# The row factors' tile moves to the place of a padding, and VectorE applies the first chunk's norm factors

## The chip, the cores and the metric

The kernel runs on one core of a Trainium2 chip. What counts is the device time of one execution in microseconds (us), as the median of several runs. One further execution was profiled.

## The reference, cut to what matters

Two transformer blocks of depth 2 are applied to 256 tokens of width 1024, all in float32. The first block normalises its input, and this is where the change to the arithmetic's place lies:

```python
def layer_norm(x, g, b):
    mu = jnp.mean(x, -1, keepdims=True)
    var = jnp.mean(jnp.square(x - mu), -1, keepdims=True)
    return (x - mu) * lax.rsqrt(var + LN_EPS) * g + b

x = layer_norm(x, ln_in_g, ln_in_b)
for l in range(DEPTH):                       # first block
    proj = einsum('bsd,de->bse', x, w_in[l]) # 1024 x 6816
    ...  # three attentions of proj's parts, gates, w_branch, w_out, layer_norm
    gu = einsum('bsd,df->bsf', x, w_ffn_in[l])
    ...  # silu(gate) * up, w_ffn_out, layer_norm
for i in range(DEPTH):                       # second block
    ...  # the same in outline: rms_norm, w_in_2, attention, gating, w_o,
    ...  # rms_norm, w_up, convolution over tokens, w_down
```

All matrix products with weights are the bulk of the work: some 257 MB of float32 weights are read once.

## The kernel before

**Matrix products.** Each weight product is done in three matmuls of a faster float32 type, on operands that are split in a high part (ScalarE casts, L188) and a low part (VectorE subtracts, L192): high with high (L254), high with low (L255), low with high (L256), all in `mm3`. The activations, turned so that the 1024 features lie on the partitions, are the tiles `xh` and `xl` (x^T, high and low), 128 x 8 x 256 elements each. The weights come by DMA into one of three `raw` tiles and are split into tiles of the pool `s4` (30 buffers of 4608 bytes a partition).

There are two kinds of product, and which operand is loaded into the array (stationary) and which streams through it (moving) differs:

- `gemm_a`: the activations are stationary (128 x 128 pieces), the weights move, 512 columns at a time (384, 288 or 256 for some narrow parts). The profile names these `ps<-s,xh` and `ps<-s,xl` where the activations are x^T, and `ps<-s,s` where they are another tile of the pool `s4` (the FFN's hidden layer, the merged attention).
- `gemm_b`: the weights are stationary, the activations move, 256 columns (all tokens) at a time. The profile names these `ps<-xh,s` and `ps<-xl,s`, or `ps<-s,s` where the activations are an attention's output in `s4` (the product with `w_branch`). Here the split weights start 64 bytes (high) or 192 bytes (low) into their `s4` buffer (`OFF_HI`, `OFF_LO`).

The order of the steps is written out by the program itself: a list of steps, each issued to the engines in turn, with the splitting of weights a fixed number of units ahead. Between the products of an attention's softmax chain, weight products are placed as filler.

**Where the tiles lie.** The pools are laid out one behind the other, and every tile starts at a multiple of 32 bytes. In the program of the kernel before, the bytes of a partition at which the tiles start are:

```
x_tok     2176     xh       10368     xl       18560     fixed    26752
pad      29376     neghalf  29408     ones     29504     col      29536
row      31328     neglam   31360     raw      31392  (and + 8192 each)
s4       55968  (and + 4608 each)     s2      194208     g, b    218784
```

`pad` is a tile of 8 floats that nothing reads or writes. `row` holds two floats a partition, the factors of the two halves of the rows in the second block's norms.

**The start.** `head` writes out the first steps: the statistics of the first 128 rows (VectorE L493, L516; GpSimd L361, L362), their norm (L523), eight transposes by TensorE (L530, two chunks of four, each chunk a PSUM bank), the cast of the first weight unit (`high(0)`, ScalarE L188), then `in_high(0, 0)`: factor and bias of the first chunk (ScalarE L537, four pieces of 128 columns) and its cast into `xh` (ScalarE L538). Only then VectorE is given the statistics of the second 128 rows (`in_stats(1)`), the low part of the first weight unit (`low_next`, L192) and that of the first chunk (`in_low(0, 0)`, L542). The same functions serve the other three chunks later.

Of the kernel before, what the change touches and what calls it, by code (L numbers as in the profile page):

```python
# [10 lines left out]
F32 = mybir.dt.float32  # L11
F32R = mybir.dt.float32r
AF = mybir.ActivationFunctionType
ALU = mybir.AluOpType
# [3 lines left out]
P = 128  # L18
# [8 lines left out]
RMS_EPS = 1e-6  # L27
MASKED = -1e30

X_PAD = 8
WARM = (0, 0)

RAW_BUFS = 3
S4_BUFS = 30
# [79 lines left out]
class Net:  # L116
# [295 lines left out]
    def constants(self):  # L412
        nc, a, cp = self.nc, self.a, self.cp
        self.x_tok = cp.tile([P, 2, D], F32, name="x_tok")
        self.xh = cp.tile([P, KT, 256], F32R, name="xh")
        self.xl = cp.tile([P, KT, 256], F32R, name="xl")
        self.fixed = cp.tile([P, a["c_fixed"].shape[1]], F32, name="fixed")
        cp.tile([P, X_PAD], F32, name="pad")
        self.neghalf = cp.tile([P, 20], F32, name="neghalf")
        nc.vector.memset(self.neghalf, -0.5)  # L420
        self.ones = cp.tile([P, 1], F32, name="ones")
        nc.vector.memset(self.ones, 1.0)
        self.col = cp.tile([P, a["c_vectors"].shape[1]], F32, name="col")
        self.row = cp.tile([P, 2], F32, name="row")
        self.neglam = cp.tile([P, DEPTH], F32, name="neglam")
        for c in range(2):
            cs = slice(c * 512, c * 512 + 512)
            nc.sync.dma_start(self.x_tok[:, 0, cs], a["x"][0, :P, cs])
        nc.sync.dma_start(self.fixed[:, :P + 2 * KT], a["c_fixed"][:, :P + 2 * KT])
        self.ident = self.fixed[:, :P]  # L430
        self.ln_in = [self.fixed[:, P + i * KT:P + (i + 1) * KT] for i in range(2)]
        o = P + 2 * KT

        def table(n):
            nonlocal o
            o += 4 * n
            return self.fixed[:, o - 4 * n:o].rearrange("p (a t n) -> p a t n", a=2, t=2)

        self.rope_df, self.rope_mla, self.rope_gqa = table(16), table(32), table(64)
        self.mask = self.fixed[:, o:o + 64]  # L440
# [91 lines left out]
    def in_high(self, t, c):  # L532
        nc, y, ps = self.nc, self.s2([P, 4, P]), self.in_ps[t, c]
        self.in_y[t, c] = y
        for k in range(4):
            g, b = (v[:, 4 * c + k:4 * c + k + 1] for v in self.ln_in)
            nc.scalar.activation(y[:, k, :], ps[:, k * P:k * P + P], AF.Identity, scale=g, bias=b)  # L537
        nc.scalar.copy(self.xh[:, 4 * c:4 * c + 4, t * P:t * P + P], y)  # L538

    def in_low(self, t, c):  # L540
        ks, ts = slice(4 * c, 4 * c + 4), slice(t * P, t * P + P)
        self.nc.vector.tensor_tensor(self.xl[:, ks, ts], self.in_y[t, c], self.xh[:, ks, ts], op=ALU.subtract)  # L542

    def warm(self, n):

        for _ in range(n):
            self.nc.tensor.matmul(self.warm_ps[:, :P], self.warm_in, self.warm_in, start=True, stop=True)

    def head(self, dfq, dfk):


        self.in_scale, self.in_ps, self.in_y = {}, {}, {}

        def first():
            if WARM[0]:
                self.warm_in, self.warm_ps = self.s2([P, P]), self.psum()
                self.nc.gpsimd.memset(self.warm_in, 1.0)
            self.warm(WARM[0])
            self.in_stats(0)
            self.in_norm(0)  # L560
            self.in_trans(0)
            self.warm(WARM[1])
            self.high(0)
            self.in_high(0, 0)
            self.in_stats(1)
            self.low_next()
            self.in_low(0, 0)
            self.high(1)
            self.low_next()
            self.in_high(0, 1)  # L570
            self.in_norm(1)
            self.in_low(0, 1)

        def second():
            self.in_trans(1)
            self.high(2)
            self.low_next()
            self.high(3)

        def third():  # L580
            self.in_high(1, 0)
            self.low_next()
            self.in_low(1, 0)
            self.in_high(1, 1)

        self.add(first, dfq[:2], second, dfq[2], third, dfq[3], lambda: self.in_low(1, 1), self.lookahead(AHEAD_EDGE), dfq[4:], dfk)

    def in_rows(self, t):
# [837 lines left out]
```

## Time and profile before

| | |
|---|---|
| median of 3 runs | 1506.68 us (1506.45 to 1506.7) |
| profiled execution | 1504.22 us, of which the span from the first to the last instruction is 1502.4 us |
| TensorE busy | 1478.0 us, 98% of the span |
| VectorE / ScalarE busy | 990.2 us (66%) / 822.8 us (55%) |
| granted TensorE clock, mean | 0.998 |

Busy time of TensorE is the time in which at least one matmul is in flight. Matmuls overlap in the pipeline, so the duration shown for one matmul is longer than the distance from its start to the next one's start; that distance is what counts where they follow one another without a wait.

### The profile page before, as it was taken

To read this page: it belongs to the slowest core of one execution; us is meant where nothing else is said; L and a number is where in the kernel's file an instruction comes from. 1 tells how busy PE (TensorE), PEld (TensorE's weight loads), DVE (VectorE), ACT (ScalarE), POOL (GpSimd) and SP (SyncE) were. 2 spreads that over 40 slices of the span, in tenths; PEclk is the share of its full clock that TensorE was granted. 3 is DMA by queue.
4 is the path that set the end of the run, shared out by engine and by line. 5 is a ranking of instruction groups with operands and counts; after the bars stand their busy time and mean duration, and the time that the engine had idled before them with its cause. 6 is when DMAs were issued, how large, how long until landed. Compare 5 with 4: busy or idle time off the path is not lost.

```text
span 1502.4 us, 23794 instructions
## 1 busy us (share of the span) xinstructions
PE 1478.0 (98%) x9616; PEld 1314.7 (88%) x9616; DVE 990.2 (66%) x1434; ACT 822.8 (55%) x1387; POOL 90.3 (6%) x116
## 2 busy tenths in 40 slices
PE   7999999999999999999999999999999999999998
PEld 5889988899988889998889998777999887789987
DVE  5786655855556676556775555876788758669881
ACT  6664566444442565656444443675767536568660
POOL 0000020000000000011000000310000012000000
PEclk9999999999999999999999999999999999999999
DMA  7744565576563654466665564553565735255660
GB/s 242 249 138 153 177 115 177 168 225 196 193 229 98 203 162 141 147 146 169 201 224 182 178 215 140 183 180 113 164 199 194 254 124 193 74 168 169 199 222 28
DMA packets 179021, 260.44 MB, mean 173 GB/s; under 512 B 23648, under 2 KB 122208, under 8 KB 178912
## 3 DMA queue, kind: packets, MB, share of 16 engines
q1 hardware_dynamic: 178912, 258.93, 54.4%
q8 instruction: 75, 1.23, 0.3%
q14 instruction: 34, 0.28, 0.1%
HBM read 257.86 MB, written 1.05 MB: 172 GB/s over the span
## 4 chain that ended last, share of the span: by engine, by line
PE 48%; DVE 3%; ACT 0%; issue 0%; POOL 0%; DVEq 0%; POOLq 0%; ACTq 0%
PE ps L254 15%; PE ps L256 15%; PE ps L255 15%; DVE s L192 1%; PE ps L1142 1%; PE ps L390 1%; PE ps L406 1%; PE ps L642 0%; DVE x_tok L505 0%; DVE st L493 0%; PE ps L1191 0%; DVE s L492 0%; PE ps L1298 0%; PE ps L1181 0%; DVE s L913 0%
## 5 line engine op out<-in xcount | busy, mean ns | idle before, releaser
L192 DVE TENSOR_TENSOR s<-raw,s 128x1024 fp32r<-128x1024 f32 (+2 forms) x468 | 553.9, 1211 | 175.4 <-ACT s L188 126.6
L188 ACT CAST s<-raw 128x1024 fp32r<-128x1024 f32 (+2 forms) x468 | 466.3, 1039 | 117.1 <-PE ps L255 26.4
L254 PE MATMUL ps<-xh,s 128*128 128x256 f32 x1664 | 475.6, 286 | 1.9 <-DVE s L738 1.4
L255 PE MATMUL ps<-xl,s 128*128 128x256 f32 x1664 | 468.0, 281 | 0.0
L256 PE MATMUL ps<-xh,s 128*128 128x256 f32 x1664 | 466.4, 280 | 0.0
L254 PEld LDWEIGHTS ps<-xh,s 128*128 128x128 f32 x1664 | 313.2, 188 | 10.1 <-issue 6.5
L255 PEld LDWEIGHTS ps<-xl,s 128*128 128x128 f32 x1664 | 317.7, 191 | 0.5
L256 PEld LDWEIGHTS ps<-xh,s 128*128 128x128 f32 x1664 | 314.0, 189 | 0.0
L254 PE MATMUL ps<-s,s 128*128 128x512 f32 (+1 forms) x712 | 259.4, 364 | 0.0
L255 PE MATMUL ps<-s,s 128*128 128x512 f32 (+1 forms) x712 | 254.6, 358 | 0.0
L256 PE MATMUL ps<-s,s 128*128 128x512 f32 (+1 forms) x712 | 254.4, 357 | 0.0
L254 PE MATMUL ps<-s,xh 128*128 128x512 f32 (+3 forms) x448 | 171.8, 383 | 3.6 <-ACT xh L538 3.2
L256 PE MATMUL ps<-s,xl 128*128 128x512 f32 (+3 forms) x448 | 169.6, 379 | 1.0 <-DVE xl L351 1.0
L255 PE MATMUL ps<-s,xh 128*128 128x512 f32 (+3 forms) x448 | 169.2, 378 | 0.0
L254 PEld LDWEIGHTS ps<-s,s 128*128 128x128 f32 x712 | 133.7, 188 | 29.2 <-issue 10.0
L256 PEld LDWEIGHTS ps<-s,s 128*128 128x128 f32 x712 | 133.7, 188 | 20.5
L255 PEld LDWEIGHTS ps<-s,s 128*128 128x128 f32 x712 | 133.8, 188 | 18.4
L254 PEld LDWEIGHTS ps<-s,xh 128*128 128x128 f32 x448 | 84.6, 189 | 20.0 <-ACT xh L538 3.6
L256 PEld LDWEIGHTS ps<-s,xl 128*128 128x128 f32 x448 | 84.5, 189 | 19.5 <-DVE xl L351 3.0
L255 PEld LDWEIGHTS ps<-s,xh 128*128 128x128 f32 x448 | 84.7, 189 | 15.8 <-DVE s L192 0.5
L361 POOL TENSOR_SCALAR st<-st 128x2 f32<-128x2 f32 (+2 forms) x46 | 24.2, 525 | 963.6 <-DVE st L500 456.9
L400 ACT ACTIVATE s<-ps,st 128x256 f32<-128x256 f32 x96 | 44.6, 472 | 50.2 <-DVE st L397 49.7
(177 smaller groups left out, 1253.6 us busy)
## 6 DMA issues: line engine op xcount, KB each, us to landing
raw<-in_w_in SPq DMA_DIRECT2D x61, 1024.0 KB, 5.2
raw<-in_w_ffn_in SPq DMA_DIRECT2D x88, 512.0 KB, 5.1
raw<-in_w_up SPq DMA_DIRECT2D x88, 512.0 KB, 5.0
raw<-in_w_ffn_out SPq DMA_DIRECT2D x22, 1024.0 KB, 5.0
raw<-in_w_down SPq DMA_DIRECT2D x22, 1024.0 KB, 5.0
raw<-in_w_branch SPq DMA_DIRECT2D x12, 1024.0 KB, 5.3
raw<-in_w_out SPq DMA_DIRECT2D x8, 1024.0 KB, 5.0
raw<-in_w_o SPq DMA_DIRECT2D x8, 1024.0 KB, 5.0
```

The source lines that it names most:

```text
L188: nc.scalar.copy(u.hi, u.raw.tile[:, u.off:u.off + u.nk, :])
L192: nc.vector.tensor_tensor(u.lo, u.raw.tile[:, u.off:u.off + u.nk, :], u.hi, op=ALU.subtract)
L254: mm(out, lh, rh, start=first, stop=False, skip_group_check=skip)
L255: mm(out, lh, rl, start=False, stop=False, skip_group_check=skip)
L256: mm(out, ll, rh, start=False, stop=last, skip_group_check=skip)
L361: self.nc.gpsimd.tensor_scalar(v, src, scale, eps, op0=ALU.mult, op1=ALU.add)
L390: self.nc.tensor.matmul(o[r, :256], vs[:, r] if vs.shape[1] == P else vs, pts[i][:, k * 256:k * 256 + 256], start=k == 0, stop=k == 1)
L400: nc.scalar.activation(p[:, qs], src[:, qs], AF.Exp, bias=nmx[:, q:q + 1], accum_out=sm[:, q:q + 1])
L406: self.nc.tensor.transpose(ps[:, k * 256 + q * P:k * 256 + q * P + P], p[:, q * 256 + k * P:q * 256 + k * P + P], self.ident)
L1142: nc.tensor.matmul(ps[:, q * 256:q * 256 + 256], S["qT"][r, h % 4, q * P:q * P + P], S["kT"][r, :], start=True, stop=True)
```

## The change

The padding tile and its size are removed, and the tile `row` is allocated where the padding was. In `in_high`, for the first chunk of the first rows alone, the factor and the bias are applied by two VectorE instructions over all 512 columns in the place of four ScalarE instructions. A function that issued warm-up matmuls, with counts of (0, 0), is removed with its constants.

```diff
-X_PAD = 8
-WARM = (0, 0)
...
         self.fixed = cp.tile([P, a["c_fixed"].shape[1]], F32, name="fixed")
-        cp.tile([P, X_PAD], F32, name="pad")
+        self.row = cp.tile([P, 2], F32, name="row")
         self.neghalf = cp.tile([P, 20], F32, name="neghalf")
...
         self.col = cp.tile([P, a["c_vectors"].shape[1]], F32, name="col")
-        self.row = cp.tile([P, 2], F32, name="row")
         self.neglam = cp.tile([P, DEPTH], F32, name="neglam")
...
     def in_high(self, t, c):
         nc, y, ps = self.nc, self.s2([P, 4, P]), self.in_ps[t, c]
         self.in_y[t, c] = y
-        for k in range(4):
-            g, b = (v[:, 4 * c + k:4 * c + k + 1] for v in self.ln_in)
-            nc.scalar.activation(y[:, k, :], ps[:, k * P:k * P + P], AF.Identity, scale=g, bias=b)
+        if t == c == 0:
+            g, b = (v[:, :4].unsqueeze(2).broadcast_to([P, 4, P]) for v in self.ln_in)
+            nc.vector.tensor_tensor(y, ps.rearrange("p (k n) -> p k n", k=4), g, op=ALU.mult)
+            nc.vector.tensor_tensor(y, y, b, op=ALU.add)
+        else:
+            for k in range(4):
+                g, b = (v[:, 4 * c + k:4 * c + k + 1] for v in self.ln_in)
+                nc.scalar.activation(y[:, k, :], ps[:, k * P:k * P + P], AF.Identity, scale=g, bias=b)
         nc.scalar.copy(self.xh[:, 4 * c:4 * c + 4, t * P:t * P + P], y)
...
-    def warm(self, n):
-        for _ in range(n):
-            self.nc.tensor.matmul(self.warm_ps[:, :P], self.warm_in, self.warm_in, start=True, stop=True)
...
-            if WARM[0]:
-                self.warm_in, self.warm_ps = self.s2([P, P]), self.psum()
-                self.nc.gpsimd.memset(self.warm_in, 1.0)
-            self.warm(WARM[0])
             self.in_stats(0)
             self.in_norm(0)
             self.in_trans(0)
-            self.warm(WARM[1])
             self.high(0)
             self.in_high(0, 0)
             self.in_stats(1)
```

## Rows read from the trace of the kernel before

**Rows 1.** Page, part 1: busy us of each engine, share of the span.

```profile
PE 1478.0 (98%) x9616; PEld 1314.7 (88%) x9616; DVE 990.2 (66%) x1434; ACT 822.8 (55%) x1387; POOL 90.3 (6%) x116
```

**Rows 2.** Matmuls of `mm3` by line and shape: count, busy us, mean ns.

```profile
L254 PE MATMUL ps<-xh,s 128*128 128x256 f32 x1664 | 475.6, 286 | 1.9 <-DVE s L738 1.4 <-ACT s L738 0.5
...
L254 PE MATMUL ps<-s,s 128*128 128x512 f32 x508 | 201.6, 397 | 0.0
...
L254 PE MATMUL ps<-s,xh 128*128 128x512 f32 x352 | 142.1, 404 | 3.6 <-ACT xh L538 3.2 <-ACT xh L350 0.4
...
L254 PE MATMUL ps<-s,s 128*128 128x256 f32 x204 | 57.8, 284 | 0.0
...
L254 PE MATMUL ps<-s,xh 128*128 128x384 f32 x32 | 10.8, 337 | 0.0
...
L254 PE MATMUL ps<-s,xh 128*128 128x288 f32 x32 | 9.5, 296 | 0.0
```

**Rows 3.** TensorE's timeline, first and last rows of four stretches: start, us, instruction.

```profile
25.77 0.39 PE L255 MATMUL ps<-s,xh 128*128 128x512 f32 x1
...
36.97 0.39 PE L255 MATMUL ps<-s,xh 128*128 128x512 f32 x1
...
258.76 0.28 PE L254 MATMUL ps<-s,s 128*128 128x256 f32 x1
...
267.94 0.28 PE L254 MATMUL ps<-s,s 128*128 128x256 f32 x1
...
379.77 0.28 PE L255 MATMUL ps<-xl,s 128*128 128x256 f32 x1
...
398.97 0.28 PE L256 MATMUL ps<-xh,s 128*128 128x256 f32 x1
...
439.73 0.39 PE L256 MATMUL ps<-s,s 128*128 128x512 f32 x1
...
469.87 0.39 PE L254 MATMUL ps<-s,s 128*128 128x512 f32 x1
```

**Rows 4.** Timeline around the largest wait of TensorE behind the start.

```profile
231.75 1.05 ACT L188 CAST s<-raw 128x1024 fp32r<-128x1024 f32 x1 [3.96 <-DMA raw<-in_w_branch]
...
234.25 0.95 PE L406 MATMUL ps<-fixed,s 128*128 128x128 f32 x4 [1.96 <-ACT s L829]
```

**Rows 5.** Windows: length, busy us of each engine, granted clock, DMA share, GB/s.

```profile
235.70:239.20 3.50, 3.50 (x15) 2.85 (x14) 0.50 (x2) 2.56 (x6) 0.76 (x1) 0.52 0.95 359
...
1060.00:1150.00 90.00, 90.00 (x768) 90.00 (x767) 74.26 (x121) 66.55 (x102) 0.00 (x0) 1.00 0.54 174
```

**Rows 6.** Timeline of the start.

```profile
6.74 1.97 PE L530 MATMUL ps<-fixed,x_tok 128*128 128x128 f32 x8 [6.74 <-DVE x_tok L523]
8.74 1.04 ACT L188 CAST s<-raw 128x1024 fp32r<-128x1024 f32 x1 [6.75 <-DMA raw<-in_w_in]
9.70 1.50 ACT L537 ACTIVATE s<-ps,fixed 128x128 f32<-128x128 f32 x4
10.03 1.29 DVE L493 BATCH_NORM_STATS2 st<-x_tok 128x6 f32<-128x512 f32 x2 [2.89 <-DMA x_tok<-in_x]
11.23 0.62 ACT L538 CAST xh<-s 128x512 fp32r<-128x512 f32 x1
...
11.48 1.18 DVE L192 TENSOR_TENSOR s<-raw,s 128x1024 fp32r<-128x1024 f32 x1
...
11.90 0.80 PE L254 MATMUL ps<-s,xh 128*128 128x512 f32 x1 [3.20 <-ACT xh L538]
12.58 0.68 DVE L542 TENSOR_TENSOR xl<-s,xh 128x512 fp32r<-128x512 f32 x1
...
12.71 0.80 PE L255 MATMUL ps<-s,xh 128*128 128x512 f32 x1
...
13.31 0.79 PE L256 MATMUL ps<-s,xl 128*128 128x512 f32 x1
```

**Rows 7.** VectorE's groups by shape: a 512-column operation with a PSUM operand.

```profile
L351 DVE TENSOR_TENSOR xl<-ps,xh 128x512 fp32r<-128x512 f32 x28 | 17.9, 683 | 11.0 <-ACT xh L350 11.0
```

## The prediction

> **What bounds the kernel now.** I read the page's busy times first: TensorE is busy for 1478.0 us, 98% of the span [rows 1]. Of the span's 1502.4 us that leaves 24.4 without a matmul, near half of it before the first product at 11.90 [rows 6]. So what changes the time by more than a few us is the distance between matmuls that follow each other without a wait, and I looked there next.
>
> The groups of matmuls by shape give the counts, and the timeline of TensorE gives the distances. In [rows 3] the reader is to divide the time from the first to the last start of a stretch by the starts in between:
>
> - weights moving, x^T stationary, 512 columns: 25.77 to 36.97 us, 49 rows, 11.20 / 48 = 233.3 ns;
> - weights moving, another `s4` tile stationary, 512 columns: 439.73 to 469.87, 134 rows, 30.14 / 133 = 226.6 ns;
> - x^T moving, weights stationary, 256 columns: 379.77 to 398.97, 164 rows, 19.20 / 163 = 117.8 ns;
> - `s4` tile moving, weights stationary, 256 columns: 258.76 to 267.94, 82 rows, 9.18 / 81 = 113.3 ns.
>
> The same instruction in the same loop is 6.7 ns (512 columns) or 4.5 ns (256 columns) slower if one of its operands is x^T. None of the four stretches has a wait, so no other engine's delay makes the difference. What differs is where the operands lie. With the starts listed above taken modulo 64 bytes, x^T lies at 0 (10368 and 18560), every `s4` buffer at 32 (55968, and 4608 is a multiple of 64), and the offsets 64 and 192 within it keep that. The two slow kinds have one operand at 0 and one at 32; the two fast kinds have both at 32. A rule that fits all four: a matmul is slower if its moving operand and the stationary operand that is loaded meanwhile are out of step by 32 bytes modulo 64.
>
> **The change part by part.**
>
> *The tile's place.* `pad` has 32 bytes; `row` has 8, and with every tile at a multiple of 32 it takes the same 32. So `neghalf`, `ones` and `col` stay. Behind `col` the old `row` is gone: `neglam` and all pools (`raw`, `s4`, `s2`, `g`, `b`, `st`) move down by 32 bytes, and `s4` starts at 55936, which is 0 modulo 64. Against x^T the `s4` buffers then lie exactly as `s4` buffers lie against one another: distance 0 modulo 512 in `gemm_a`, 64 and 192 in `gemm_b`, the distances of the two fast stretches. So I forecast that matmuls with x^T take the fast distances:
>
> - 256 columns, x^T moving: 1664 on each of three lines [rows 2], 4992 x 4.5 ns = 22.5 us;
> - 512 columns, x^T stationary: 352 x 3 = 1056 x 6.7 ns = 7.1 us;
> - the narrow ones (384 and 288 columns, 32 x 3 each [rows 2], and a third narrow kind about as many): 288 matmuls; no stretch shows their fast form, so between nothing and 6.7 ns each, 0 to 1.9 us; I take 1.2, since they lie between the two widths whose gains are 4.5 and 6.7.
>
> The products of `s4` with `s4` keep their distance modulo 512 and so their pace.
>
> From this 30.8 us something is given back. Filler between the steps of a softmax chain gets shorter, and where the chain or a transfer is what ends last, the wait grows. [rows 4] show such a place: ScalarE stood 3.96 us for a weight transfer, and TensorE behind it 1.96 us. About 1,540 of the 4,992 matmuls lie in the attentions, worth 6.9 us; I take 2 us of it as lost, between 0 and all 6.9. Elsewhere the engines that feed TensorE have room: in the densest stretch of the second block's FFN VectorE is busy 74.26 of 90 us [rows 5], 82.5%, and the same work in 4% less time would be 86%.
>
> Here a rule speaks against this part. The Trainium skill (TensorE: Matmul & The Clock Gate, section "Step-by-step: what each phase is for") says that TensorE reads moving and stationary operands through two independent ports and that loading the next weights takes nothing from the running matmul. By that rule the operands' places don't matter and this part would be worth 0. The trace disagrees as far as the 226.6 against 233.3 ns above show; what no row shows is a matmul with both operands at 0.
>
> *Factor and bias by VectorE.* Removed: four ScalarE instructions, 1.50 us. Added: two on VectorE over 512 columns, one with a PSUM operand, at 0.683 us each [rows 7], 1.37 us. In the start [rows 6] ScalarE takes them up behind the weight cast, 9.70 to 11.20, then the cast into `xh`, 0.62, and TensorE starts its first product at 11.90. After the change VectorE can start when the first chunk's transposes end (about half of 6.74 to 8.71, so 7.7) and is done near 9.1; ScalarE casts `xh` right behind the weight cast, 9.8 to 10.4, and the first matmul starts near 10.45, 1.45 us earlier. But the second matmul (L255) needs the low part of the weights, which VectorE makes from 11.48 to 12.66, and the third (L256) the low part of the chunk, ready at 13.26. Both stand on VectorE behind the statistics of the second rows, which wait for a transfer that lands at 10.03. That chain doesn't move. So L255 stays at 12.71, L256 at 13.31, and what follows with them: worth 0. The two new instructions are hidden by VectorE's idle 2.89 us before 10.03; with that cover gone they would cost 1.37. ScalarE is free 1.5 us earlier for the second weight unit, whose low part still waits for VectorE. Bounds: 1.45 us gained to 1.37 lost.
>
> *The warm-up function* issued nothing at counts of (0, 0): 0.
>
> **Sum.** 22.5 + 7.1 + 1.2 - 2.0 + 0 = 28.8 us less. The profiled execution took 1504.22 us (1502.4 of span), 2.5 us under the median of the runs, 1506.68; the sum is a difference and I set it against the median: 1477.9, told as 1478. One thing of that size is in neither: a stretch at half clock (0.52 granted in 235.70 to 239.20 [rows 5], and a second like it near 700 us), behind waits as in [rows 4]. 3.5 us at half the rate cost 1.75; none, one or three of them may be left.
>
> **The rivals.**
>
> *The place doesn't matter.* x^T matmuls are slow for a reason that moves with x^T. For it: the rule of two ports, named above, and that no x^T operand is seen at another place. Against it: the pairs differ in nothing else, and `s4` buffers far apart and close together all have the fast distance. Then all that is left is the start: 1506.7 less 0 to 1.45, about 1506.4.
>
> *Slower: a start at 0 modulo 64 is itself what costs.* The four stretches are fitted by a second rule too: fast only if no operand lies at 0. Then after the change every operand lies there; x^T matmuls gain nothing, and the products of `s4` with `s4` fall to the slow distances: 508 x 3 x 6.7 ns = 10.2 us and 204 x 3 x 4.5 ns = 2.8 us [rows 2], so 1506.7 + 13.0 = 1519.7. It decides as soon as the 512-column products of the FFN's second half stand at 233 ns. For it: no matmul of these rows has both at 0. Against it: two reads that disturb each other should depend on their distance, and moving both by 32 bytes leaves that as it is.
>
> **How the numbers follow.** The forecast has 0.68, no effect of the place 0.13, the slower rule 0.19. Under about 0.2% (3 us) a measurement of this kernel tells nothing from no change; the start alone stays under that. So faster 0.68, same 0.13, slower 0.19. The forecast's own range is 1472 (all 30.8 us kept, both half-clock stretches gone: 1506.7 - 30.8 - 3.5) to 1485 (all 6.9 us of the attentions lost and one more half-clock stretch: 1477.9 + 4.9 + 1.75). To leave out no more than 2 in 10, the range takes in the case of no effect: 1472 to 1507.
>
> **What would show it.** Right: from start to start, 256-column matmuls with x^T near 113.3 ns and 512-column ones near 226.6, `s4` products unchanged; the first L254 near 10.45 us with L255 still near 12.7; the DVE chain from 10.03 unmoved. Wrong: x^T matmuls still at 117.8 and 233.3 (place without effect), or `s4` products at 233 (the second rule), or fast matmuls with TensorE's waits risen by as much as they gained (a chain or the transfers bound it). If L255 starts with L254 near 11, the low part didn't wait as I read it.

## The result, and the profile after

The changed kernel took 1483.10 us (median of 3 runs, 1482.66 to 1484.14) against 1506.68: a ratio of 0.9845, 95% interval 0.9823 to 0.9868. The forecast was 1478, in the range of 1472 to 1507. The profiled execution took 1484.14 us with a span of 1482.3, against 1504.22 and 1502.4 before: 20.1 us less in this pair of profiles, 23.6 us in the medians. The working below explains the pair of profiles. Executions of one kernel spread with TensorE's granted clock: the 55 runs of the kernel before in the experiments below took 1500.2 to 1503.9 us where its mean was 0.999 or more, and 1506.5 to 1511.5 us where it was 0.995, so that a difference of 2 or 3 us between medians of a few runs tells little.

First the page's busy times and its group of 256-column products with x^T moving (count, busy us, mean ns):

```profile
PE 1453.9 (98%) x9616; PEld 1294.3 (87%) x9616; DVE 989.4 (67%) x1436; ACT 820.8 (55%) x1383; POOL 90.2 (6%) x116
...
L250 PE MATMUL ps<-xh,s 128*128 128x256 f32 x1664 | 467.0, 281 | 1.9 <-DVE s L729 1.4
```

The same 9616 matmuls keep TensorE busy for 24.1 us less than in [rows 1], and the group's mean fell from 286 to 281 ns [rows 2]. That mean mixes waits and pace, so the timeline is needed. First and last rows of the four kinds of stretch, as in [rows 3] (start, us, instruction; `mm3`'s lines are now 250 to 252):

```profile
257.74 0.28 PE L250 MATMUL ps<-s,s 128*128 128x256 f32 x1
...
266.92 0.28 PE L250 MATMUL ps<-s,s 128*128 128x256 f32 x1
...
292.24 0.39 PE L250 MATMUL ps<-s,xh 128*128 128x512 f32 x1
...
297.00 0.39 PE L250 MATMUL ps<-s,xh 128*128 128x512 f32 x1
...
379.81 0.28 PE L250 MATMUL ps<-xh,s 128*128 128x256 f32 x1
...
398.96 0.28 PE L251 MATMUL ps<-xl,s 128*128 128x256 f32 x1
...
438.66 0.39 PE L250 MATMUL ps<-s,s 128*128 128x512 f32 x1
...
468.81 0.39 PE L251 MATMUL ps<-s,s 128*128 128x512 f32 x1
```

From start to start: `s4` tile moving 9.18 / 81 = 113.3 ns (82 rows; as before), x^T stationary 4.76 / 21 = 226.7 (22 rows; before 233.3), x^T moving 19.15 / 169 = 113.3 (170 rows; before 117.8), `s4` stationary 30.15 / 133 = 226.7 (134 rows; as before). The x^T products of these two shapes have taken the pace of the others, and the products of `s4` with `s4` kept theirs. With this the rival of no effect (117.8 and 233.3 left) and the slower rival (`s4` products at 233 with a start at 0 modulo 64) are both out.

Both profiles issue the same matmuls in the same order, so each distance from one start to the next can be paired with its counterpart, and the changes summed by kind:

| kind of distance | us | forecast |
|---|---|---|
| x^T moving, 256 columns (4845 at a steady pace, 89 beside waits or at half clock) | -21.7 | -22.5 |
| x^T stationary, 512 columns, steady (982) | -5.7 | -7.1 |
| x^T stationary, 384, 288 and 256 columns, steady (272) | 0.0 | -1.2 |
| `s4` with `s4` (2083) | -0.1 | 0 |
| last weight product to the next transposes, score products or transposes among themselves | +6.2 | +2.0 |
| first product 1.9 earlier, x^T's 512-column products beside waits 2.1 later | +0.2 | 0 |
| rest (from x^T products to the step behind them, above all the token mixing of the second block) | +1.0 | 0 |
| sum | -20.1 | -28.8 |

The narrow kinds did move, in both directions: 384 columns from 175.0 to 173.9 ns, 288 from 133.4 to 132.4, 256 from 116.8 to 119.1.

One pair of profiles is one execution of each kernel. Four more profiles of kernels with the same pace (the changed kernel again, and place alone, all at 32 and 256 up of the experiments below) were paired with the same profile of the kernel before. The first two lines hold: 20.7 to 22.1 us and 5.6 to 5.7 us less. The +6.2 is the largest of the five: it is +2.9 for the changed kernel's second profile, and +4.9, +4.5 and +2.5 for the other three. The sums are 21.0 to 23.9 us less.

Where the +6.2 arises is seen in TensorE's list of waits (engine, line, releaser: us in all, times, longest) and in the timeline around the largest of them:

```profile
PE ps L402 <- ACT s L820: 7.6, 5, 2.9
```

```profile
229.95 1.04 ACT L184 CAST s<-raw 128x1024 fp32r<-128x1024 f32 x1 [4.30 <-DMA raw<-in_w_branch]
...
231.89 0.91 ACT L820 ACTIVATE s<-s,st 128x256 f32<-128x256 f32 x2
...
232.45 1.30 PE L402 MATMUL ps<-fixed,s 128*128 128x128 f32 x4 [2.85 <-ACT s L820]
...
236.84 1.28 POOL L843 TENSOR_TENSOR s<-s,fixed 128x512 f32<-128x512 f32 x1 [7.52 <-DMA s<-in_na_rpb]
...
238.16 0.69 DVE L854 TENSOR_TENSOR s<-ps,s 128x512 f32<-128x512 f32 x1 [3.49 <-POOL s L843]
```

It is the place of [rows 4]. ScalarE's wait for the weights grew from 3.96 to 4.30 us, TensorE's behind it from 1.96 to 2.85, and GpSimd waits 7.52 us for the attention's bias table `na_rpb`, and VectorE, which adds it to the scores, 3.49 us for GpSimd. All waits on this line came to 3.6 us (2 times) before and to 7.6 (5 times) now; in the four other profiles they came to 5.4 to 6.3. The half clock behind it, two stretches of 3.5 us before [rows 5], is one of 6.9 us (columns as in [rows 5]):

```profile
233.00:239.90 6.90, 6.90 (x27) 5.73 (x28) 3.35 (x6) 3.56 (x9) 1.28 (x1) 0.52 0.66 238
```

The timeline of the start, to be laid beside [rows 6]:

```profile
7.47 1.04 ACT L184 CAST s<-raw 128x1024 fp32r<-128x1024 f32 x1 [5.48 <-DMA raw<-in_w_in]
7.83 0.69 DVE L533 TENSOR_TENSOR s<-ps,fixed 128x512 f32<-128x512 f32 x1 [0.75 <-PE ps L526]
8.56 0.69 DVE L534 TENSOR_TENSOR s<-s,fixed 128x512 f32<-128x512 f32 x1
9.17 1.28 DVE L489 BATCH_NORM_STATS2 st<-x_tok 128x6 f32<-128x512 f32 x2
9.28 0.62 ACT L539 CAST xh<-s 128x512 fp32r<-128x512 f32 x1 [0.76 <-DVE s L534]
9.95 0.80 PE L250 MATMUL ps<-s,xh 128*128 128x512 f32 x1 [1.30 <-ACT xh L539]
...
11.84 0.80 PE L251 MATMUL ps<-s,xh 128*128 128x512 f32 x1 [1.09 <-DVE s L188]
```

The first product starts at 9.95 us in the place of 11.90, and TensorE then waits 1.09 us for the low part of the weights. VectorE takes up the statistics of the second rows (L489) directly behind its two new instructions (L533, L534).

### The profile page after: what moved, and what is told of

Same layout as the page of the kernel before. It is cut to its first block, busy times and chain, and to the rows that moved or that the text cites. A ratio compares the mean times of both kernels' runs of the same rounds, so it can differ in the third digit from the quotient of the medians.

```text
span 1482.3 us, 23794 instructions
## 1 busy us (share of the span) xinstructions
PE 1453.9 (98%) x9616; PEld 1294.3 (87%) x9616; DVE 989.4 (67%) x1436; ACT 820.8 (55%) x1383; POOL 90.2 (6%) x116
## 2 busy tenths in 40 slices
DMA packets 179021, 260.44 MB, mean 176 GB/s; under 512 B 23648, under 2 KB 122208, under 8 KB 178912
## 4 chain that ended last, share of the span: by engine, by line
PE 48%; DVE 3%; ACT 1%; issue 1%; DMA 0%; POOL 0%; DVEq 0%; ACTq 0%; POOLq 0%
PE ps L250 15%; PE ps L252 15%; PE ps L251 14%; PE ps L1133 1%; DVE s L188 1%; PE ps L386 1%; PE ps L402 1%; PE ps L633 0%; DMA raw<-in_w_in 0%; DVE x_tok L501 0%; PE ps L1182 0%; PE ps L1289 0%; PE ps L1172 0%; ACT s L184 0%; DVE s L904 0%
## 5 line engine op out<-in xcount | busy, mean ns | idle before, releaser
L250 PE MATMUL ps<-xh,s 128*128 128x256 f32 x1664 | 467.0, 281 | 1.9 <-DVE s L729 1.4
L252 PE MATMUL ps<-xh,s 128*128 128x256 f32 x1664 | 460.7, 277 | 0.0
L251 PE MATMUL ps<-xl,s 128*128 128x256 f32 x1664 | 460.6, 277 | 0.0
L251 PEld LDWEIGHTS ps<-xl,s 128*128 128x128 f32 x1664 | 313.5, 188 | 0.5
L251 PE MATMUL ps<-s,s 128*128 128x512 f32 (+1 forms) x712 | 254.6, 358 | 0.0
L250 PE MATMUL ps<-s,xh 128*128 128x512 f32 (+3 forms) x448 | 170.1, 380 | 1.7 <-ACT xh L539 1.3
L251 PE MATMUL ps<-s,xh 128*128 128x512 f32 (+3 forms) x448 | 167.4, 374 | 1.1 <-DVE s L188 1.1
L251 PEld LDWEIGHTS ps<-s,s 128*128 128x128 f32 x712 | 133.8, 188 | 18.4
L251 PEld LDWEIGHTS ps<-s,xh 128*128 128x128 f32 x448 | 84.8, 189 | 15.0 <-DVE s L188 1.6
```

The lines of the kernel that those rows point to most:

```text
L250: mm(out, lh, rh, start=first, stop=False, skip_group_check=skip)
L251: mm(out, lh, rl, start=False, stop=False, skip_group_check=skip)
L252: mm(out, ll, rh, start=False, stop=last, skip_group_check=skip)
```

## The experiments

Times are medians; each ratio is to the kernel before on the same chip, in the same batch, with its 95% interval. The kernel before took 1505.34, 1505.21 and 1506.15 us in the three batches (17, 23 and 15 runs between 1500.2 and 1511.5). Diffs are against the changed kernel, unless said.

**1. The two parts apart, and the changed kernel again** (batch 1). The place alone, with `in_high` as before:

```diff
-        if t == c == 0:
...
+        for k in range(4):
+            g, b = (v[:, 4 * c + k:4 * c + k + 1] for v in self.ln_in)
+            nc.scalar.activation(y[:, k, :], ps[:, k * P:k * P + P], AF.Identity, scale=g, bias=b)
```

> The changed kernel with the first chunk's factor and bias back on ScalarE: the row factors' place alone. If the distance between x^T and the s4 buffers makes the gain: 1483 us, give or take 1.5, with the 256-column matmuls of x^T 113.3 ns and the 512-column ones 226.6 ns from start to start. If VectorE's part makes it: near 1506 us with 117.8 and 233.3 ns.

Measured: 1483.19 us, 0.9851 (0.9831 to 0.9871); distances with x^T 113.5 and 226.8 ns.

VectorE's part alone, with padding and `row` where they were:

```diff
-        self.row = cp.tile([P, 2], F32, name="row")
+        cp.tile([P, X_PAD], F32, name="pad")
...
         self.col = cp.tile([P, a["c_vectors"].shape[1]], F32, name="col")
+        self.row = cp.tile([P, 2], F32, name="row")
```

> The kernel before, padding and all, with the first chunk's factor and bias on VectorE: the other part alone. If the distance makes the gain: 1506.7 us, give or take 1.5, with 117.8 and 233.3 ns. If VectorE's part makes it: near 1483 us.

Measured: 1506.89 us, 1.0008 (0.9994 to 1.0021); distances 117.9 and 233.4 ns.

The changed kernel again:

> The changed kernel once more, on the chip of the two halves, so that the VectorE part can be read as its difference to the place alone. By the prediction's reading of the start (the second matmul waits for the low part of the weights, which VectorE makes in the same chain) that difference is within 0.5 us; the other reading, that the first matmul's earlier start is kept, gives 1 to 1.5 us less than the place alone.

Measured: 1480.68 us, 0.9832 (0.9815 to 0.9848). The place has the whole gain. VectorE's part can't be told from nothing: alone its interval is 0.9 us less to 3.2 more, and the intervals with and without it beside the place overlap. There the medians differ by 2.5 us, more than either reading had forecast; the two profiles put 2.0 us of their difference on waits behind other steps, as in the +6.2 above, and 0.6 on the start.

**2. Every start at 32 modulo 64** (batch 1). A tile of 32 bytes ahead of x^T moves x^T to 10400 and 18592 and `s4` to 55968, where it lay before:

```diff
         self.x_tok = cp.tile([P, 2, D], F32, name="x_tok")
+        cp.tile([P, 8], F32, name="shift")
         self.xh = cp.tile([P, KT, 256], F32R, name="xh")
```

> The changed kernel with 32 bytes left free ahead of xh, so that x^T and all pools start at 32 modulo 64 and keep their distances. If the distance counts: 1483 us, give or take 1.5, with 113.3 and 226.6 ns. If what counts is that the s4 buffers start at 0 modulo 64 when x^T is the other operand: near 1506 us with 117.8 and 233.3 ns.

Measured: 1483.57 us, 0.9851 (0.983 to 0.9873); 113.5 and 227.2 ns. Since `raw` and `s4` are where they were before and the gain is kept, no address by itself makes it, neither of the matmuls' operands nor of the DMA's target. What counts is the distance between x^T and the pools.

**3. Which operand: half of the weights moved by 32 bytes** (batch 2). In `gemm_b` alone, first the low part of the weights, then the high part:

```diff
-OFF_HI, OFF_LO = 16, 48
+OFF_HI, OFF_LO = 16, 56
```

> The changed kernel with the low weights of gemm_b starting 224 bytes into their buffer in the place of 192, so 32 modulo 64, while everything else stays at 0. If a matmul is slowed by the operand that is loaded while it runs: in gemm_b only the distance from L251 to L252 grows (while L251 runs, the low weights are loaded), 113.3 to about 118 ns, 1856 times 4.5 to 5.5 ns or 8 to 10 us: 1491 to 1493 us. If it is slowed by its own stationary operand: only the distance from L252 to the next L250 grows. If gemm_b's distance over 64 bytes is of no effect: 1483 us.

Measured: 1500.4 us, 0.9963 (0.9946 to 0.9981); 256 columns, x^T moving 117.1 ns, `s4` tile moving 117.1; `gemm_a`, which has no such offsets, 226.8.

```diff
-OFF_HI, OFF_LO = 16, 48
+OFF_HI, OFF_LO = 24, 48
```

> The changed kernel with the high weights of gemm_b starting 96 bytes into their buffer in the place of 64, so 32 modulo 64. If the operand that is loaded meanwhile counts: the distances from L250 and from L252 grow (the high weights are loaded while both run) and that from L251 stays at 113.3 ns; 1856 times 8 to 9 ns, 15 to 17 us: 1498 to 1500 us. If a matmul's own stationary operand counts: those from L250 and L251 grow, that from L252 stays.

Measured: 1500.51 us, 0.9969 (0.9952 to 0.9986); 117.8 ns for both kinds of `gemm_b`, 226.8 for `gemm_a`. So the penalty can be switched on for products of `s4` with `s4` too. But it falls on all three lines (medians 117 to 118 ns each with the low part moved), not on the one line whose own stationary operand was moved, nor only on the one that streams while that operand is loaded. With the low part moved most of the gain is gone, 1500.4 us, where one slower line alone would have left 1491 to 1493. Neither pairing is shown.

**4. The period: pools moved up by 64, 128 and 256 bytes** (64 in batch 2, the others, with 32 and 64 floats in the tile, in batch 3):

```diff
         self.neglam = cp.tile([P, DEPTH], F32, name="neglam")
+        cp.tile([P, 16], F32, name="shift")
         for c in range(2):
```

> The changed kernel with 64 bytes left free behind neglam, so that all pools lie 64 bytes higher. If only the distance modulo 64 counts: 1483 us, give or take 1.5, with 113.3 and 226.6 ns. If the distances 0, 64 and 192 themselves are the good ones (now 64, 128 and 256): x^T matmuls somewhere between 113.3 and 118 ns or 226.6 and 233.3 ns, and a time between 1485 and 1506 us.

Measured: 1507.04 us, 1.0004 (0.9987 to 1.002). The gain is gone, although every distance is still a multiple of 64. TensorE's timeline, x^T moving, first and last of 163 rows:

```profile
379.73 0.28 PE L250 MATMUL ps<-xh,s 128*128 128x256 f32 x1
...
398.90 0.28 PE L250 MATMUL ps<-xh,s 128*128 128x256 f32 x1
```

19.17 / 162 = 118.3 ns; x^T stationary 228.8, `s4` with `s4` 113.7 and 226.8.

> The changed kernel with 128 bytes left free behind neglam. If the pace follows the distance over a period of 128 bytes: 113.3 and 226.6 ns and about 1482 us. If over 256 or 512 bytes: x^T matmuls off these, 1490 to 1507 us.

Measured: 1502.89 us, 0.9983 (0.9963 to 1.0003). The first and last of 171 rows in the FFN of the first layer, then of 170 rows in the second block:

```profile
379.73 0.28 PE L252 MATMUL ps<-xh,s 128*128 128x256 f32 x1
...
399.00 0.28 PE L251 MATMUL ps<-xl,s 128*128 128x256 f32 x1
...
1089.83 0.28 PE L250 MATMUL ps<-xh,s 128*128 128x256 f32 x1
...
1109.92 0.28 PE L251 MATMUL ps<-xl,s 128*128 128x256 f32 x1
```

19.27 / 170 = 113.4 ns, but 20.09 / 169 = 118.9: the same loop, on tiles at the same distances, has the fast pace in the first of four such stretches and the slow one in the other three. x^T stationary stood at 232.4 to 233.2. At the start of the first stretch the pace even changes from one to the other, behind four transposes:

```profile
316.80 0.28 PE L250 MATMUL ps<-xh,s 128*128 128x256 f32 x1
...
322.03 0.28 PE L252 MATMUL ps<-xh,s 128*128 128x256 f32 x1
322.15 0.60 PE L991 MATMUL ps<-fixed,s 128*128 128x128 f32 x4
...
323.30 0.28 PE L250 MATMUL ps<-xh,s 128*128 128x256 f32 x1
...
325.90 0.28 PE L252 MATMUL ps<-xh,s 128*128 128x256 f32 x1
```

The 45 rows ahead of the transposes give 5.23 / 44 = 118.9 ns, the 24 from 323.30 on 2.60 / 23 = 113.0. This profile has 56 runs of 19 or more such matmuls without a break: from the seventh matmul on 42 of them are slow and 14 fast, and none changes. In the profile of the kernel before all 56 are slow. So at the distances of this kernel the place alone does not settle the pace: it is settled as a run begins and then kept; by what, no run shows.

> The changed kernel with 256 bytes left free behind neglam. If the pace follows the distance over a period of 128 or 256 bytes: 113.3 and 226.6 ns and about 1482 us. If over 512 bytes (the s4 buffers among themselves lie at multiples of 512 and have the fast pace): x^T matmuls off these, 1490 to 1507 us.

Measured: 1482.37 us (2 runs), 0.9845 (0.9816 to 0.9874); the timeline of its stretch, first and last of 170 rows:

```profile
379.75 0.28 PE L252 MATMUL ps<-xh,s 128*128 128x256 f32 x1
...
398.90 0.28 PE L250 MATMUL ps<-xh,s 128*128 128x256 f32 x1
```

19.15 / 169 = 113.3 ns, x^T stationary 226.7: the gain is whole again. All kernels, by the distance from the start of the x^T tile to that of the weights' tile, modulo 256 bytes:

| kernel | `gemm_a` | `gemm_b`, high and low | x^T stationary, ns | x^T moving, ns |
|---|---|---|---|---|
| before | 32 | 96, 224 | 233.3 | 117.8 |
| changed; place alone; all at 32; 256 up | 0 | 64, 192 | 226.7 to 227.2 | 113.3 to 113.5 |
| 64 up | 64 | 128, 0 | 228.8 | 118.3 |
| 128 up | 128 | 192, 64 | 232.4 to 233.2 | 113.4 or 118.9 |
| low part at 32 | 0 | 64, 224 | 226.8 | 117.1 |
| high part at 32 | 0 | 96, 192 | 226.8 | 117.8 |

**5. Where the rest of the gain went: the bias table** (1 KB pieces in batch 2, runs in batch 3). The table's shifted windows are read in pieces of 256 bytes, 23648 packets under 512 bytes in the page's DMA part of the changed kernel. In the first kernel as many bytes come from `w_out`, in pieces of 1 KB, to the same tiles; it leaves out the bias table and so computes something else:

```diff
...
-                    nc.sync.dma_start(b[r * 64:r * 64 + 64, q, :].rearrange("p (r c) -> p r c", r=4),
-                                        bass.AP(tensor=rpb.tensor, offset=o, ap=[[1, 64], [31, 4], [1, 64]]))
+                    nc.sync.dma_start(b[r * 64:r * 64 + 64, q, :], a["w_out"][l][h * P + r * 64:h * P + r * 64 + 64, q * 256:q * 256 + 256])
```

> The changed kernel with the neighbourhood attention's bias taken from rows of w_out in pieces of 1 KB in the place of pieces of 256 bytes of na_rpb: the same bytes, buffers and semaphores, other values, so the output isn't the reference's. If TensorE's waits for the softmax chain there (L402 behind L820, 7.6 us in the changed kernel, 3.6 before) come from transfers slowed by the small pieces: these waits fall under 3 us and the time to 1476 to 1480 us. If the chain of the softmax itself, or the order in which the queue issues, sets them: 7 to 8 us of waits and 1483 us.

Measured: 1471.35 us (1470.82 to 1472.5), 0.9767 (0.9746 to 0.9788), 5 us below the range expected; 7264 packets under 512 bytes, and the wait of L402 is no longer among the largest.

The second kernel computes all that the changed one does. Each partition's four overlapping windows are one run of 157 floats in memory; it is loaded once, and GpSimd picks the windows out of it while it adds the mask (`S4_BUFS` is 29 in the place of 30, for the room):

```diff
...
+                    nc.sync.dma_start(run[r * 64:r * 64 + 64, q, :157], bass.AP(tensor=rpb.tensor, offset=o, ap=[[1, 64], [1, 157]]))
...
+            for q in range(2):
+                v = b[:, q, :].rearrange("p (r c) -> p r c", r=4)
+                w = bass.AP(tensor=run.tensor, offset=run.offset + q * 160, ap=[list(run.ap[0]), [31, 4], [1, 64]])
+                nc.gpsimd.tensor_tensor(v, w, self.mask.unsqueeze(1).broadcast_to([P, 4, 64]), op=ALU.add)
```

> The changed kernel with the neighbourhood attention's bias loaded as one run of 157 floats (628 bytes) for each partition and query half, 256 pieces for each head in the place of 1024 of 256 bytes; GpSimd picks the four rows of 64 out of the run while it adds the mask, in two instructions in the place of one; one s4 buffer less makes room for the runs. The values are the reference's. If the small pieces slow the transfers there, most of what pieces of 1 KB brought (1471.35 us) comes back: 1470 to 1475 us, with TensorE's waits for the softmax chain (L402) under 3 us. If it was GpSimd's or VectorE's chain, or the bytes: near 1482 us.

Measured: 1474.75 us (1473.28 to 1475.89), 0.9796 (0.9777 to 0.9814), faster than both kernels of the case. DMA issues between 200 and 240 us (median us from issue to landing last), of the changed kernel and then of this one:

```profile
raw<-in_w_branch SPq DMA_DIRECT2D x2, 1024.0 KB, 12.2
s<-in_na_rpb SPq DMA_DIRECT2D x16, 64.0 KB, 11.2
```

```profile
raw<-in_w_branch SPq DMA_DIRECT2D x2, 1024.0 KB, 5.5
run<-in_na_rpb SPq DMA_DIRECT2D x10, 39.2 KB, 4.6
```

In the kernel before these two took 11.2 and 8.6 us. The small pieces hold up the weights in the same queue. With faster matmuls the table's landing took longer still, by 2.6 us here and by less over all 32 transfers of the layer (median 8.0 us before, 9.0 now). Without the small pieces weights and table land in half the time and TensorE's waits on L402 go. It isn't the bytes, since the first kernel moves as many; whether it is the pieces' size, their number or that they all read one small table, the two kernels don't separate.

## Why the prediction came out as it did

**What bounds the kernel, and the place.** Right: the pace of the matmuls set the time, and the place of the operands the pace. The Trainium skill (TensorE: Matmul & The Clock Gate, "Step-by-step: what each phase is for") says that moving and stationary operands are read through two independent ports. The prediction's rival took from it that places don't matter; experiments 1 and 2 show that they do for this kernel's matmuls, with 113.5 against 117.9 ns by the place of a tile alone. Whether it is these two reads that disturb each other, no run here shows.

**The rule behind it.** "Out of step by 32 bytes modulo 64" fitted all four stretches of [rows 3] and is wrong: with the pools 64 bytes up it would have kept the gain, and the kernel took 1507.04 us. The distances repeat with 256 bytes, not 64. The forecast held because it said more than the rule needed: that x^T and `s4` would lie as `s4` buffers lie among themselves, the same modulo 512. The other half of the rule, that it is the stationary operand loaded meanwhile, is not borne out by experiment 3, and no other pairing took its place.

**The terms.** 256 columns: 22.5 forecast, 21.7 measured. 512 columns: 7.1 forecast, 5.7 measured; the 982 steady distances gave 5.8 ns each where the stretch of [rows 3] had promised 6.7. The narrow products gave nothing where 1.2 was forecast: interpolating between two widths was no ground. Width alone can't be it, since 256 columns with x^T moving took the fast pace and 256 with x^T stationary got 2.3 ns slower; the cause stays open.

**What is given back.** Right in place and mechanism, too small in size: 2.0 forecast, 6.2 in the pair above and 2.5 to 4.9 in the four others, all inside the bound of 6.9. [rows 4] showed the late weights, but the forecast took TensorE's 1.96 us for the whole of the matter and did not follow GpSimd, which stood for the bias table. Experiment 5 shows the cause: without the small pieces the kernels take 1471.35 and 1474.75 us against 1480.68 to 1483.10, 6 to 12 us less. The waits (7.6 us) and the half clock behind them (6.9 us at half the rate, 3.5) are 11 together, by estimate. Part of that price the kernel before paid already.

**The start.** Forecast 0, measured 0.2. As expected the first product comes earlier and the second does not follow by as much: L251 starts at 11.84 us, L255 did at 12.71 [rows 6]. These 0.87 us come from the transfer: L251 starts 2.7 to 3.1 us behind the landing of the second rows of x, which came at 10.01 us before, at 9.89, 9.37 and 9.11 in experiment 1 (L251's counterpart at 12.60, 12.07 and 11.91) and at 8.78 here. Here it is 3.06 us in the place of 2.70: the two new instructions ended at 9.25, 0.5 us after the rows were there. The cover named in the forecast was thus nearly, not fully, there. In all thirteen profiles L251, or its counterpart, starts 2.7 us behind the start of the second rows' statistics, so the chain is as it was read and only its start moved. Little of the 0.87 us lasts: TensorE reaches the next eight transposes at 16.88 us, while its products are still 0.43 us apart, they take 1.50 us in the place of 1.03, and the product behind them starts at 18.13, before at 18.30.

**The sum.** 28.8 forecast, 20.1 in the profiles and 23.6 in the medians. Of the 8.7 between forecast and profiles, 4.2 are waits, 3.4 the three terms of pace, 1.2 the start and the rest. Of these the pace is the steady part; with the changed kernel's second profile (23.7 us less) the waits miss by 0.9 alone. That the median came within 5.1 us of the forecast owes nothing to errors that cancel: every term came out smaller than forecast or cost more.

**What stays open.** Which two accesses disturb each other (for `gemm_b` the weights' place alone is enough, for `gemm_a` the pools were only moved all together); what decides between the two paces when the set 64 and 192 is swapped between high and low part, in the kernel 128 up; why narrow products don't gain; what VectorE's part is worth, +1.6 us by the medians alone and -2.5 beside the place, neither clear of the spread.

## What to carry to other kernels

Divide long stretches without a wait into time per matmul, for each pair of operands; where the same shape has two paces, compare the tiles' start addresses, and lay a slow pair out at distances that a fast pair already has, to the full period and not to the smallest that fits the rows. A 32-byte tile moved was worth 1.5% here. And when the bounding engine gets faster, follow the largest waits back to their transfers first: many small pieces in the queue of the weights took back a tenth to a quarter of what the pace gave (2.5 to 6.2 of some 27 us). One pair of profiles doesn't size such a wait: take a second profile of the same kernel before explaining it.

## What the runs showed of the hardware that was not expected

The pace of a matmul of this type depends on the distance within a partition from the start of the x^T tile to that of the weights' tile. Of shifts by 32, 64, 128 and 256 bytes only the last left the pace as it was: 113.3 to 118.9 ns for 256 columns and 226.7 to 233.3 for 512, with a value between (228.8) at 64. One layout held both paces, in different stretches of one execution and on either side of four transposes, and none of its 56 unbroken runs changed pace. And 256-byte pieces, 1.6% of all bytes (23648 less 7264 packets of 256 bytes, 4.2 of 260 MB), went with twice the landing time of the weights beside them (12.2 against 5.5 us).
